# Stick-breaking scores: query parts stacked in the rows of one product, the third product side by side

## The chip, the core and the metric

The kernel runs on one core of a Trainium2 chip. What counts is its device time in microseconds (us). The time before is the median of three runs, 755.0 us (754.8 to 755.26). One further run was taken with the hardware profiler; its rows are quoted below. Engines: PE is the matrix engine (PEld is its weight loads, which overlap its products), DVE, ACT and POOL work on tiles elementwise, and SP issues most DMAs.

## The reference, cut to what matters

One decoder layer on 512 tokens and 1024 features: a norm, one wide projection, two attentions, a merge, an output projection and an FFN. The change concerns the scores of the stick-breaking attention: 8 heads of 64 features.

```python
z = jnp.einsum('bhqd,bkhd->bhqk', q_blk, k, preferred_element_type=jnp.float32) * scale
causal = kpos[None, :] < tpos[:, None]
log_keep = jnp.where(causal, jax.nn.log_sigmoid(-z), 0.0)
log_after = lax.cumsum(log_keep, axis=3, reverse=True) - log_keep
a = jnp.where(causal, jnp.exp(jax.nn.log_sigmoid(z) + log_after), 0.0)
return jnp.einsum('bhqk,bkhd->bqhd', a.astype(v.dtype), v)
```

## The kernel before

Nearly every product is made of three: a float32 operand is split into a high part in a rounded type (`float32r`) and a low part that holds the rest, and high*high, high*low and low*high are summed in PSUM (`mm3`, L161). A weight chunk of 128 x 1024 is loaded by SP, its high part is made by a copy on ACT (L147) and its low part by a subtraction on DVE (L148).

The projections come first in PE's program. `proj_feature` (L370) makes 128 features of all 512 tokens from 24 products of 512 columns, and DVE evicts them from PSUM at once (L379 and L381). `proj_token` (L384) makes values by token; for 512 columns it has four banks, two of them an "attention pair" (`take`) and two of the tag "proj". The order of the chunks is written at L644 to L659: `vs` (the values), q and k of head pair 1, of head pair 2, the six dilated chunks of the first dilated pair (`project_dil(0)`), q and k of head pair 3, then `vd0`, `vd12`, six more dilated chunks and sixteen gate chunks.

The attention runs beside this as generators that `tick` resumes after every three products. `sb_all` (L603) takes the four head pairs one after the other; each starts when its k is there and the pair ahead is through. In `sb_pair` (L436) a pair has three score groups: x (key blocks 1 and 3: 384 and 128 columns), y (key block 2: 256 columns) and z (key block 0: 512 columns). `scores` takes one of three attention pairs of PSUM banks and computes the group for both heads of the pair as plain float32 products (L441): head 0 has its 64 features in rows 0 to 63 of q and k, head 1 in rows 64 to 127, so each product uses 64 rows of the array. A mask product over all 128 rows follows (L445). `breaks` is a chain on two engines: absolute value, exponential and logarithm on ACT (L452 to L454), a sum on DVE (L455), the high part by a copy on ACT (L174) and the low part on DVE (L175). `weigh` (L469) multiplies both parts with a triangle (L472) on PE into the same banks and takes the exponential on ACT, which frees the banks; `side` (L477) multiplies with the values. POOL sums over partitions (L464) beside it. The dilated attention starts when all four pairs are done.

Each engine works through its instructions in a fixed order. Within the limits of data and buffers that order is chosen when the program is built, from priorities and an estimate of durations; q, k and the dilated chunks share 16 buffers (`NQ`).

Of the kernel before, what the change touches and what calls it, by code (L numbers as in the profile page):

```python
# [10 lines left out]
F32 = mybir.dt.float32  # L11
F32R = mybir.dt.float32r
BF16 = mybir.dt.bfloat16
AF = mybir.ActivationFunctionType
ALU = mybir.AluOpType

P = 128
S = 512
# [9 lines left out]
RAW, NQ, N4, N2, NS = 3, 16, 9, 6, 4  # L28
# [16 lines left out]
def trunk_kernel(ctx, tc, xT, gains, w_in, w_up, w_o, w_f, w_d, bias, out):  # L45
# [6 lines left out]
    V, A, G, T = nc.vector, nc.scalar, nc.gpsimd, nc.tensor  # L52
# [13 lines left out]
    def bank(tag, name):  # L66
        if tag == "proj":
            return pp.tile([P, S], F32, tag=tag, name=name, bufs=BANKS[tag])
        if ppool[1] is not None:
            return ppool[1].tile([P, S], F32, tag="att" if tag == "alpha" else "sums", name=name, bufs=BANKS["att"])  # L70
        return pair(name)[:, 0, :]
# [24 lines left out]
    for step in FFN:  # L96
        if step[0] == "in":
            i = step[1]
            chunks += [("A1", w_f[2 * i], 1024), ("S23", w_f[2 * i + 1], 1024), ("S1", None, 1024), ("S4", None, 512)]
        else:  # L100
            _, p, f = step
# [96 lines left out]
    ap_ = attp.__enter__()  # L198
# [29 lines left out]
    for k in range(KD):  # L228
# [8 lines left out]
        lo = xp.tile([P, S], F32R, tag=f"xl{k}", name=f"xl{k}")  # L237
# [5 lines left out]
    with tc.high_priority():  # L243
        weights(0)
        tc.add_manual_dep(state["last"].ins, last_split.ins.name, NOSYNC, reason="issue order")
        for x in xw:
            i = A.activation(x, x, AF.Square)
# [4 lines left out]
        V.tensor_tensor(out=xw[0], in0=xw[0], in1=xw[2], op=ALU.add)  # L252
        V.tensor_tensor(out=acc1, in0=xw[0][:, 0, :], in1=xw[0][:, 1, :], op=ALU.add)


    ident = cp.tile([P, P], F32)
    make_identity(nc, ident)
# [51 lines left out]
    def can_take():  # L309
        return min(free) <= ticks[0]  # L310
# [44 lines left out]
    def next_weights(ahead=2):  # L355
        w = weights(ci[0], ahead)
        ci[0] += 1
        return w

    def product(ps, mh_, ml_, w, nk, first=True, last=True, k0=0, between={}):  # L360
        hi, lo = w
        for k in range(nk):
            cs = slice(k * P, (k + 1) * P)
            mm3(ps, hi[:, cs], lo[:, cs], mh_[k0 + k], ml_[k0 + k], first and k == 0, last and k == nk - 1)
            tick()
            if k in between:
                with tc.high_priority():
                    between[k]()

    def proj_feature(name, scale=None, ps=None, blocks=False):  # L370
        if ps is None:
            ps = bank("proj", f"pj{name}")
            product(ps, xh, xl, next_weights(), KD)
        rb = rows["rb"]
        o = ap_.tile([P, S], F32, tag="qk", name=name, bufs=NQ)
        view = (lambda t, out=False: t.rearrange("p (c i) -> p i c" if out else "p (i c) -> p i c", c=4)) if blocks else (lambda t, out=False: t)
        with tc.high_priority():
            if scale is None:
                V.tensor_tensor(out=view(o, True), in0=view(ps), in1=view(rb), op=ALU.mult)  # L379
            else:  # L380
                V.scalar_tensor_tensor(out=view(o, True), in0=view(ps), scalar=scale, in1=view(rb), op0=ALU.mult, op1=ALU.mult)  # L381
        return o

    def proj_token(name, kind, wide_, pairs=0):  # L384

        v = ap_.tile([P, 4, wide_], F32, tag=name, name=name)
        nk = 1024 // wide_
        if wide_ == 512:
            banks = []
            for i in range(pairs):  # L390
                while not can_take():
                    tick()
                p = take(f"pv{name}{i}")
                banks += [p[:, 0, :], p[:, 1, :]]
            banks += [bank("proj", f"pv{name}{c}") for c in range(len(banks), 4)]
        else:

            b2 = [bank("proj", f"pv{name}{c}") for c in range(2)]
            banks = [b2[c // 2][:, c % 2 * wide_:(c % 2 + 1) * wide_] for c in range(4)]
        w = {}  # L400
        for j, c in [(j, c) for j in range(KD // nk) for c in range(4)]:
            if j not in w:
                w[j] = next_weights()
            ps = banks[c]
            whi, wlo = w[j]
            for i in range(nk):
                k = j * nk + i
                cs = slice(i * wide_, (i + 1) * wide_)
                mm3(ps, blk(xh[k], kind, c), blk(xl[k], kind, c), whi[:, cs], wlo[:, cs], k == 0 and (wide_ == 512 or c % 2 == 0), k == KD - 1, check=wide_ == 512)
                tick()  # L410
            if j == KD // nk - 1 and (wide_ == 512 or c % 2):
                with tc.high_priority():
                    for cc in [c] if wide_ == 512 else [c - 1, c]:
                        A.mul(v[:, cc, :], banks[cc], rows["r1"][:, 4 * kind + cc:4 * kind + cc + 1])
        for i in range(pairs if wide_ == 512 else 0):
            give(4)
        return v
# [9 lines left out]
        split_to(hi, lo, src)  # L427
        o_hi[i], o_lo[i] = hi, lo

    hs = [slice(0, 64), slice(64, 128)]  # L430

# [1 line left out]
    def sb_pair(n, q, k, v, hb, done):  # L436
        def scores(name, parts):
            ps = take(f"z{n}{name}")
            for i, (a, o) in enumerate(parts):
                for h in range(2):  # L440
                    T.matmul(ps[:, h, o:o + S - a * P], k[hs[h], a * P:(a + 1) * P], q[hs[h], a * P:], start=i == 0, stop=False, skip_group_check=True)  # L441
            for h in range(2):
                diag = ps[:, h, :].rearrange("p (a b) -> p a b", b=P)
                diag = diag[:, 0:4:3, :] if len(parts) == 2 else diag[:, 0:1, :]
                T.matmul(diag, idb, mask[:, :len(parts)], start=False, stop=False, skip_group_check=True)  # L445
            return ps
# [66 lines left out]
        f = wide(f"f{n}").rearrange("p a b -> p (a b)")[:, 256:1024]  # L513
# [3 lines left out]
        o = small(f"o{n}")  # L517
# [81 lines left out]
    vals = {}  # L599
# [18 lines left out]
            yield from dil_pair(n, [vals[f"dq{n}{g}"] for g in range(3)], [vals[f"dk{n}{g}"] for g in range(3)], lambda: vals.get("vd"))  # L618

    def project(n):  # L620
        vals[f"q{n}"] = proj_feature(f"sq{n}", 0.125)
        vals[f"k{n}"] = proj_feature(f"sk{n}")

    def project_dil(n):
        for g in range(3):
            vals[f"dq{n}{g}"] = proj_feature(f"dq{g}{n}", 0.125, blocks=g > 0)
            vals[f"dk{n}{g}"] = proj_feature(f"dk{g}{n}", blocks=g > 0)

# [2 lines left out]
    first = [pf[:, i, :] for i in range(2)]  # L631
    w = [next_weights(1 - i) for i in range(2)]
# [5 lines left out]
    def first_steps():  # L638
        yield from row_steps()
        give(3)  # L640
        vals["q0"] = proj_feature("sq0", 0.125, first[0])
        vals["k0"] = proj_feature("sk0", None, first[1])

    start(first_steps(), 14)  # L644
    start(sb_all())
    start(dil_all())
    vals["vs"] = proj_token("vs", 0, 512, 1)
    project(1)
    project(2)
    project_dil(0)  # L650
    project(3)
    vd = [proj_token("vd0", 0, 256)]
    v12 = proj_token("vd12", 1, 512, 1)
# [25 lines left out]
    for f in range(KD):  # L679
# [11 lines left out]
        lo = xp.tile([P, S], F32R, tag=f"xl{f}", name=f"ml{f}")  # L691
# [14 lines left out]
    hs = S // 2  # L706
# [35 lines left out]
    for f in HALVES:  # L742
        x = res(f)
        ps = bank("proj", f"po{f}")
# [221 lines left out]
def _layout(inputs, np):  # L966
    def feature(w, cols):
        k = w.shape[0] // P
        return w[:, cols].reshape(k, P, P).transpose(1, 0, 2).reshape(P, k * P)

    def token(w, wide):
        n = D * wide // (P * 1024)
        return list(w.reshape(n, D // (P * n), P, wide).transpose(0, 2, 1, 3).reshape(n, P, 1024))

    def fb(c0, i):
        return slice(c0 + i * P, c0 + (i + 1) * P)

    w = inputs["w_in"][0]
    ch = []
    def sb(n):  # L980
        return [feature(w, fb(0, n)), feature(w, fb(512, n))]

    def dil(n):
        return [feature(w, fb(c, 2 * g + n)) for g in range(3) for c in (1536, 2304)]

    ch += sb(0) + token(w[:, 1024:1536], 512) + sb(1) + sb(2) + dil(0) + sb(3)
    ch += token(w[:, 3072:3328], 256) + token(w[:, 3328:3840], 512) + dil(1)
    for f in range(KD):
        ch.append(feature(w, fb(3840, f)))
        ch.append(feature(w, fb(4864, f)))  # L990
    wf, wd = inputs["w_ffn_in"][0], inputs["w_ffn_out"][0]
    fch = []
    for i in range(KF):
        fch.append(feature(wf, fb(0, i)))
        fch.append(feature(wf, fb(DFF, i)))
    up = [np.concatenate([feature(inputs["w_sb_up"][0], fb(0, f)), feature(inputs["w_dil_up"][0], fb(0, f))], axis=1) for f in range(KD)]
    gains = [inputs[n].reshape(KD, P).transpose(1, 0) for n in ("norm_mix_g", "norm_ffn_g", "norm_final_g")]
    return {
        "in_xT_dram": inputs["x"][0].transpose(1, 0).reshape(KD, P, S),
        "in_gains_dram": np.concatenate(gains, axis=1),  # L1000
        "in_w_in_dram": np.stack(ch),
        "in_w_up_dram": np.stack(up),
        "in_w_out_dram": np.stack([feature(inputs["w_out"][0], fb(0, f)) for f in range(KD)]),
        "in_w_ffn_in_dram": np.stack(fch),
        "in_w_ffn_out_dram": np.stack([feature(wd, fb(0, f)) for f in range(KD)]),
    }
# [35 lines left out]
```

## Time and profile before

| | |
|---|---|
| median of three runs | 755.0 us |
| profiled execution, device time | 755.51 us |
| its span (first to last instruction) | 753.8 us |
| PE busy | 744.0 us of the span |
| DVE busy | 523.3 us |
| ACT busy | 364.9 us |
| POOL busy | 79.9 us |
| granted PE clock, mean | 0.998 of full |

The profiled execution spends 1.7 us outside its span. In a row of the timeline stand the start in us, the time from the first start to the last end in us, the engine, the line, the operation, output and inputs, the shape and the number of instructions merged. PE's products are pipelined: a row's duration holds the fill and drain, and what one costs is read from start to start.

### The profile page before, as it was taken

To read this page: it belongs to the slowest core of one execution; us is meant where nothing else is said; L and a number is where in the kernel's file an instruction comes from. 1 tells how busy PE (TensorE), PEld (TensorE's weight loads), DVE (VectorE), ACT (ScalarE), POOL (GpSimd) and SP (SyncE) were. 2 spreads that over 40 slices of the span, in tenths; PEclk is the share of its full clock that TensorE was granted. 3 is DMA by queue.
4 is the path that set the end of the run, shared out by engine and by line. 5 is a ranking of instruction groups with operands and counts; after the bars stand their busy time and mean duration, and the time that the engine had idled before them with its cause. 6 is when DMAs were issued, how large, how long until landed. Compare 5 with 4: busy or idle time off the path is not lost.

```text
span 753.8 us, 10956 instructions
## 1 busy us (share of the span) xinstructions
PE 744.0 (99%) x4447; PEld 644.2 (85%) x4447; DVE 523.3 (69%) x685; ACT 364.9 (48%) x526; POOL 79.9 (11%) x48
## 2 busy tenths in 40 slices
PE   9999999999999999999999999999999999999996
PEld 6877767788887888888888999999999999999985
DVE  6447657535887763376998989878788777776643
ACT  7255746743233533232564666545445454444453
POOL 1004043150150130000000000000000000000033
PEclk9999999999999999999999999999999999999999
DMA  8321211213232232234222233223333333332213
GB/s 266 125 83 63 79 57 57 84 56 140 85 115 110 87 110 97 70 113 159 102 75 85 92 98 105 98 84 120 99 105 98 106 99 102 106 108 70 57 57 113
DMA packets 25187, 74.13 MB, mean 98 GB/s; under 512 B 2864, under 2 KB 5936, under 8 KB 25008
## 3 DMA queue, kind: packets, MB, share of 16 engines
q1 hardware_dynamic: 23664, 69.74, 28.1%
q0 software_dynamic: 784, 3.15, 1.2%
q8 instruction: 35, 0.57, 0.3%
q10 hardware_dynamic: 688, 0.54, 0.2%
q14 instruction: 16, 0.13, 0.1%
HBM read 71.32 MB, written 2.10 MB: 97 GB/s over the span
## 4 chain that ended last, share of the span: by engine, by line
PE 93%; DVE 2%; DMA 2%; ACT 1%; issue 1%; SPq 0%; POOLq 0%; POOL 0%; DVEq 0%; ACTq 0%
PE pd L163 16%; PE pjgs L163 6%; PE pjgd L163 6%; PE pf L789 5%; PE pf L790 5%; PE pf L791 5%; PE pvvd L163 5%; PE pjdq L163 4%; PE pjdk L163 4%; PE po L163 4%; PE pg L789 4%; PE pg L790 4%; PE pg L791 4%; PE up L163 4%; PE pvvs L163 3%; PE pjsq L163 2%
## 5 line engine op out<-in xcount | busy, mean ns | idle before, releaser
L147 ACT CAST whi<-raw 128x1024 fp32r<-128x1024 f32 (+2 forms) x114 | 108.6, 954 | 160.6 <-PE pg L790 34.6
L148 DVE TENSOR_TENSOR wlo<-raw,whi 128x1024 fp32r<-128x1024 f32 (+2 forms) x114 | 138.1, 1213 | 39.9 <-ACT whi L147 39.1
L789 PE MATMUL pf<-fh,whi 128*128 128x256 f32 x348 | 98.9, 284 | 1.3 <-ACT q L796 1.3
L791 PE MATMUL pf<-fh,wlo 128*128 128x256 f32 x348 | 98.6, 283 | 0.0
L790 PE MATMUL pf<-fl,whi 128*128 128x256 f32 x348 | 98.5, 283 | 0.0
L789 PE MATMUL pg<-fh,whi 128*128 128x256 f32 x264 | 75.1, 285 | 0.6 <-ACT q L796 0.6
L790 PE MATMUL pg<-fl,whi 128*128 128x256 f32 x264 | 74.7, 283 | 0.0
L791 PE MATMUL pg<-fh,wlo 128*128 128x256 f32 x264 | 74.7, 283 | 0.0
L789 PEld LDWEIGHTS pf<-fh,whi 128*128 128x128 f32 x348 | 66.7, 192 | 2.6 <-ACT q L796 1.9
L790 PEld LDWEIGHTS pf<-fl,whi 128*128 128x128 f32 x348 | 66.7, 192 | 0.6
L791 PEld LDWEIGHTS pf<-fh,wlo 128*128 128x128 f32 x348 | 66.7, 192 | 0.3 <-DVE wlo L148 0.2
L148 DVE TENSOR_TENSOR wlo<-s,whi 128x1024 fp32r<-128x1024 f32 (+1 forms) x43 | 41.3, 960 | 15.3 <-ACT whi L147 15.2
L147 ACT CAST whi<-s 128x1024 fp32r<-128x1024 f32 (+1 forms) x43 | 36.2, 841 | 32.3 <-PE pg L790 20.5
L789 PEld LDWEIGHTS pg<-fh,whi 128*128 128x128 f32 x264 | 50.6, 192 | 1.1 <-ACT q L796 0.8
L790 PEld LDWEIGHTS pg<-fl,whi 128*128 128x128 f32 x264 | 50.7, 192 | 0.0
L791 PEld LDWEIGHTS pg<-fh,wlo 128*128 128x128 f32 x264 | 50.7, 192 | 0.0
L163 PE MATMUL pd<-hh,whi 128*128 128x512 f32 (+1 forms) x132 | 50.4, 382 | 0.0
L163 PE MATMUL pd<-hl,whi 128*128 128x512 f32 (+1 forms) x132 | 50.3, 381 | 0.0
L163 PE MATMUL pd<-hh,wlo 128*128 128x512 f32 (+1 forms) x132 | 50.1, 379 | 0.0
L892 POOL TENSOR_TENSOR inv<-inv,sq 128x256 f32<-128x256 f32 (+1 forms) x10 | 9.6, 962 | 318.1 <-ACT sq L891 315.8
L886 DVE TENSOR_TENSOR res<-pd,res 128x512 f32<-128x512 f32 (+1 forms) x36 | 22.6, 629 | 20.9 <-PE pd L163 20.8
L147 ACT CAST whi<-rawu 128x1024 fp32r<-128x1024 f32 x22 | 23.1, 1050 | 27.9 <-PE pd L163 23.7
(463 smaller groups left out, 1791.0 us busy)
## 6 DMA issues: line engine op xcount, KB each, us to landing
raw<-in_w_in_dram SPq DMA_DIRECT2D x43, 512.0 KB, 3.3
rawu<-in_w_ffn_in_dram SPq DMA_DIRECT2D x22, 512.0 KB, 3.2
raw<-in_w_ffn_in_dram SPq DMA_DIRECT2D x22, 512.0 KB, 3.3
raw<-in_w_ffn_out_dram SPq DMA_DIRECT2D x24, 384.0 KB, 3.1
raw<-in_w_out_dram SPq DMA_DIRECT2D x8, 512.0 KB, 3.3
raw<-in_w_up_dram SPq DMA_DIRECT2D x8, 384.0 KB, 2.9
x<-in_xT_dram SPq DMA_DIRECT2D x8, 256.0 KB, 4.7
res<-in_xT_dram POOLq DMA_DIRECT2D x8, 256.0 KB, 4.5
```

The source lines that it names most:

```text
L147: state["last"] = A.copy(hi[:, cs], r[:, cs])
L148: V.tensor_tensor(out=lo[:, cs], in0=r[:, cs], in1=hi[:, cs].bitcast(F32), op=ALU.subtract)
L163: return T.matmul(ps, a, b, start=start, stop=stop, skip_group_check=not check)
L789: T.matmul(ps, hi[:, cs], xhi, start=first and k == 0, stop=False, skip_group_check=True)
L790: T.matmul(ps, hi[:, cs], xlo, start=False, stop=False, skip_group_check=True)
L791: T.matmul(ps, lo[:, cs], xhi, start=False, stop=last and k == 3, skip_group_check=True)
L886: newest[1] = V.tensor_tensor(out=x, in0=ps, in1=x, op=ALU.add)
L892: G.tensor_tensor(out=rows["inv"][:, cs], in0=rows["inv"][:, cs], in1=sq[:, cs], op=ALU.add)
```

## The change

After `proj_feature` a new function `scored` makes operands of the rounded type. For q it makes two tiles, one for each head: in the head's own 64 rows the high part of q, in the other 64 rows the low part. For k it makes two tiles with the high part of the head in both halves of the rows, and one tile with the low parts of both heads. One product over 128 rows then gives k high * (q high + q low) for one head; a third product, over the 64 rows of the head, adds k low * q high. The four projections with their high and low copies add, for a head pair, four copies on ACT, two copies and four subtractions on DVE, each of 64 rows and 512 columns. Also, four of the six dilated chunks are moved ahead of q and k of pair 2, in the order of the code and in the order of the weights.

```diff
+    def scored(t, key):
+        lo = ap_.tile([P, S], F32R, tag="qk", name="klow", bufs=NQ) if key else None
+        tiles = []
+        with tc.high_priority():
+            for h in range(2):
+                own, other = hs[h], hs[1 - h]
+                y = ap_.tile([P, S], F32R, tag="qk", name=f"{'kq'[not key]}{h}", bufs=NQ)
+                A.copy(y[own], t[own])
+                if key:
+                    V.tensor_copy(y[other], y[own])
+                V.tensor_tensor(out=lo[own] if key else y[other], in0=t[own], in1=y[own].bitcast(F32), op=ALU.subtract)
+                tiles.append(y)
+        return tiles + [lo]
...
             for i, (a, o) in enumerate(parts):
                 for h in range(2):
-                    T.matmul(ps[:, h, o:o + S - a * P], k[hs[h], a * P:(a + 1) * P], q[hs[h], a * P:], start=i == 0, stop=False, skip_group_check=True)
+                    T.matmul(ps[:, h, o:o + S - a * P], k[h][:, a * P:(a + 1) * P], q[h][:, a * P:], start=i == 0, stop=False, skip_group_check=True)
+                for h in range(2):
+                    T.matmul(ps[:, h, o:o + S - a * P], k[2][hs[h], a * P:(a + 1) * P], q[h][hs[h], a * P:], start=False, stop=False, skip_group_check=True)
...
-        vals[f"q{n}"] = proj_feature(f"sq{n}", 0.125)
-        vals[f"k{n}"] = proj_feature(f"sk{n}")
-
-    def project_dil(n):
-        for g in range(3):
+        vals[f"q{n}"] = scored(proj_feature(f"sq{n}", 0.125), False)
+        vals[f"k{n}"] = scored(proj_feature(f"sk{n}"), True)
+
+    def project_dil(n, groups=range(3)):
+        for g in groups:
...
-        vals["q0"] = proj_feature("sq0", 0.125, first[0])
-        vals["k0"] = proj_feature("sk0", None, first[1])
+        vals["q0"] = scored(proj_feature("sq0", 0.125, first[0]), False)
+        vals["k0"] = scored(proj_feature("sk0", None, first[1]), True)
...
     project(1)
+    project_dil(0, [0, 1])
     project(2)
-    project_dil(0)
+    project_dil(0, [2])
     project(3)
...
-    ch += sb(0) + token(w[:, 1024:1536], 512) + sb(1) + sb(2) + dil(0) + sb(3)
+    d0 = dil(0)
+    ch += sb(0) + token(w[:, 1024:1536], 512) + sb(1) + d0[:4] + sb(2) + d0[4:] + sb(3)
```

What this does to the engines' orders is seen at three places.

**PE, scores of pair 0.** Before, they stand behind the 23rd of the 24 products that project q of pair 1 (`pjsq`); `sq` and `sk` are q and k of pair 0, and x2 is one row for the two heads.

```order
L163 MATMUL pjsq_436<-xl_172,whi_339 128x512
L441 MATMUL z0x<-sq_394,sk_396 128x384 x2
L441 MATMUL z0x<-sq_394,sk_396 128x128 x2
L445 LDWEIGHTS idb
L445 MATMUL z0x<-mask,idb 128x2x128
```

Now they begin behind the 16th product of the next chunk (`pjsk`, k of pair 1). `q_396` and `k_405` are the stacked tiles of head 0, `q_399` and `k_409` those of head 1; L458 is a product over 128 rows, L460 one over 64.

```order
L458 MATMUL z0x<-q_396,k_405 128x384
L458 MATMUL z0y<-q_396,k_405 128x256
L458 MATMUL z0z<-q_396,k_405 128x512
L163 MATMUL pjsk_530<-xl_160,whi_378 128x512
L458 MATMUL z0x<-q_399,k_409 128x384
L460 MATMUL z0x<-q_396,klow 128x384
L458 MATMUL z0y<-q_399,k_409 128x256
L460 MATMUL z0x<-q_399,klow 128x384
L458 MATMUL z0x<-q_396,k_405 128x128
L458 MATMUL z0x<-q_399,k_409 128x128
L460 MATMUL z0x<-q_396,klow 128x128
L460 MATMUL z0x<-q_399,klow 128x128
```

So the scores stand 17 products of 512 columns later, and those of pair 0 are cut apart: products over 128 and over 64 rows alternate, and those over 64 rows of x and 384 columns stand alone instead of in pairs. In pairs 1 to 3 a group stands together, as two products over 128 rows and two over 64.

**PE, the last group of pair 3.** Before, 78 rows, all products, lie between the mask of z3z and the first product that needs its high part, h3z. The piece begins with the second mask product of z3z.

```order
L445 MATMUL z3z<-mask,idb 128x128
L163 MATMUL pvvd_1069<-whi_1026,xh_159 128x256
L163 MATMUL pvvd_1069<-wlo_1027,xh_159 128x256
L163 MATMUL pvvd_1069<-whi_1026,xl_160 128x256
L163 MATMUL pvvd_1069<-whi_1026,xh_165 128x256
```

The same queue further on, around h3z and l3z (`pvvd` is the token projection, `tri` the triangle):

```order
L163 MATMUL pvvd_1272<-whi_1276,xh_159 128x512
L472 MATMUL z3z<-h3z,tri 128x512 x2
L163 MATMUL pvvd_1272<-wlo_1277,xh_159 128x512
L163 MATMUL pvvd_1272<-whi_1276,xl_160 128x512
L163 MATMUL pvvd_1273<-wlo_1277,xh_153 128x512
```

Now, from the second mask product of z3z:

```order
L464 MATMUL z3z<-mask,idb 128x128
L491 MATMUL z3x<-l3x,tri 128x512 x2
L163 MATMUL pvvd_1365<-whi_1368,xh_159 128x512
L163 MATMUL pvvd_1365<-wlo_1369,xh_159 128x512
L163 MATMUL pvvd_1365<-whi_1368,xl_160 128x512
L491 MATMUL z3y<-h3y,tri 128x256 x2
L491 MATMUL z3y<-l3y,tri 128x256 x2
L491 MATMUL z3z<-h3z,tri 128x512 x2
L491 MATMUL z3z<-l3z,tri 128x512 x2
L163 MATMUL pvvd_1363<-whi_1157,xh_129 128x512
```

Nine products are left between the mask and h3z. The rest of the token projection `vd12` that comes behind (`pvvd_1363`) goes into the attention pair of banks, of which z3x, z3y and z3z hold all three.

**DVE, the operands of pair 0.** Before, between the eviction of k of pair 0 and that of q of pair 1:

```order
L379 TENSOR_TENSOR sk_396<-first,rb_392 128x512
L148 TENSOR_TENSOR wlo_440<-raw_337,whi_439 128x1024
L381 SCALAR_TENSOR_TENSOR sq_499<-pjsq_436,rb_392 128x512
L148 TENSOR_TENSOR wlo_505<-raw_376,whi_504 128x1024
L455 SCALAR_TENSOR_TENSOR t0x<-z0x,t0x 128x1024
```

Now:

```order
L381 TENSOR_TENSOR sk_402<-first,rb_392 128x512
L148 TENSOR_TENSOR wlo_459<-raw_337,whi_458 128x1024
L399 TENSOR_TENSOR q_396<-sq_394,q_396 64x512
L399 TENSOR_TENSOR q_399<-sq_394,q_399 64x512
L398 COPY k_405<-k_405 64x512
L399 TENSOR_TENSOR klow<-sk_402,k_405 64x512
L398 COPY k_409<-k_409 64x512
L399 TENSOR_TENSOR klow<-sk_402,k_409 64x512
L383 SCALAR_TENSOR_TENSOR sq_522<-pjsq_455,rb_392 128x512
```

Six instructions of 64 rows stand between one split of weights and the next eviction; the scores of the pair wait for them. On PE everything behind the dilated chunks stands in the same order as before.

More of the change, by code (lines that the diff above doesn't have):

```diff
@@ L253, in trunk_kernel @@
         V.tensor_tensor(out=acc1, in0=xw[0][:, 0, :], in1=xw[0][:, 1, :], op=ALU.add)
+    hs = [slice(0, 64), slice(64, 128)]
     ident = cp.tile([P, P], F32)
@@ L428, in split_out @@
         o_hi[i], o_lo[i] = hi, lo
-    hs = [slice(0, 64), slice(64, 128)]
     def sb_pair(n, q, k, v, hb, done):
```

## The prediction

> **What bounds the kernel now.** I read the page first, then who waited for whom on PE, then the two stretches in which the attention runs beside the projections.
>
> ```profile
> PE 744.0 (99%) x4447; PEld 644.2 (85%) x4447; DVE 523.3 (69%) x685; ACT 364.9 (48%) x526; POOL 79.9 (11%) x48
> PE 93%; DVE 2%; DMA 2%; ACT 1%; issue 1%; SPq 0%; POOLq 0%; POOL 0%; DVEq 0%; ACTq 0%
> PE pf L789 <- ACT q L796: 1.3, 2, 0.9
> PE warm L80 <- DVE warm L77: 1.0, 1, 1.0
> PE pg L789 <- ACT q L796: 0.6, 1, 0.6
> PE first L163 <- DVE xl L187: 0.3, 1, 0.3
> 43.00:98.00 55.00, 55.00 (x263) 41.10 (x262) 35.24 (x36) 35.48 (x44) 14.49 (x3) 1.00 0.20 67
> 98.00:170.00 72.00, 72.00 (x385) 56.55 (x384) 38.70 (x42) 43.24 (x60) 23.73 (x7) 1.00 0.20 66
> ```
>
> PE is the bound: 93% of the chain that ended last is PE, and in the list of waits (us in total, times, longest) no score, triangle or value product stands. In the two stretches, which hold all of the stick-breaking attention, PE is busy throughout while DVE has 35.2 of 55 and 38.7 of 72 us, ACT 35.5 and 43.2. So every us of PE work added or saved here, and every new wait of PE, is a us of the result; copies on DVE and ACT are free as long as PE finds its operands ready.
>
> **What the scores cost.** The stretch of pair 0 with the last of the projection around it:
>
> ```profile
> 43.03 0.39 PE L163 MATMUL pjsq<-xh,whi 128*128 128x512 f32 x1
> ...
> 48.02 0.39 PE L163 MATMUL pjsq<-xl,whi 128*128 128x512 f32 x1
> 48.34 1.14 PE L441 MATMUL z0x<-sq,sk 64*128 64x384 f32 x8
> 49.41 0.39 PE L445 MATMUL z0x<-mask,idb 128*128 128x256 bf16 x2
> 49.73 0.70 PE L441 MATMUL z0y<-sq,sk 64*128 64x256 f32 x4
> 50.37 0.28 PE L445 MATMUL z0y<-mask,idb 128*128 128x128 bf16 x2
> 50.59 1.13 PE L441 MATMUL z0z<-sq,sk 64*128 64x512 f32 x4
> 51.65 0.28 PE L445 MATMUL z0z<-mask,idb 128*128 128x128 bf16 x2
> 51.74 0.48 PE L163 MATMUL pjsq<-xh,wlo 128*128 128x512 f32 x1
> 52.06 0.39 PE L163 MATMUL pjsk<-xh,whi 128*128 128x512 f32 x1
> ```
>
> A rounded product of 512 columns costs 0.227 us (22 steps in 48.02 - 43.03), 0.44 ns a column. The float32 group z0z of 512 columns takes 1.06 (50.59 to 51.65), z0y of 256 takes 0.64: 0.42 for 256 columns more, 1.64 ns a column with both heads side by side, and 0.22 fixed. Entry adds 0.09: 48.34 is 0.32 behind the product of 48.02, not 0.227. So a stretch over 64 rows costs its columns plus 0.31: weights that can't be loaded ahead (about 0.11), and a drain on each side. And a rounded product behind a mask starts its successor 0.32 later (51.74 to 52.06): 0.09 for weights not loaded ahead. Pair 0 thus cost 1.16 for x (48.25 to 49.41), 0.73 for y, 1.15 for z: 3.04 us.
>
> With the change the columns are cheap and the stretches are not. x: two products of 384 (0.34), a stretch over 64 rows (0.31 + 0.17), 0.10 for weights again, two products of 128 columns that wait for their weights (0.16), a second stretch (0.31 + 0.06): 1.45. y: 0.24 + 0.31 + 0.11 = 0.66. z: 0.45 + 0.31 + 0.22 = 0.98. Sum 3.09, against 3.04: what four passes less save goes into one more stretch over 64 rows and into products that change between 128 and 64 rows. Four pairs: +0.2. Pair 0 is cut apart besides: the two lone products of 384 columns make one stretch more (0.31), return to 128 rows once more (0.10) and don't share their columns (0.17): +0.6. Mask products ahead of stacked ones add 0.09 twice. Value products (L479) stand in seven groups instead of eight, some of them right beside scores; a group has the same 0.3 of changes, so -0.3. **PE's own work: +0.7 us.** The ends are -0.5 (all joined groups save, pair 0 costs nothing extra) and +1.5.
>
> **The operands.** 16 copies on ACT, 8 copies and 16 subtractions on DVE.
>
> ```profile
> L515 ACT ACTIVATE f<-s2x 64x512 f32<-64x512 f32 x2 | 1.3, 628 | 0.0
> L175 DVE TENSOR_TENSOR ols<-o,ohs 128x512 fp32r<-128x512 f32 x4 | 2.8, 690 | 2.4 <-ACT ohs L174 2.4
> 44.89 1.23 DVE L148 TENSOR_TENSOR wlo<-raw,whi 128x1024 fp32r<-128x1024 f32 x1 [1.04 <-ACT whi L147]
> ```
>
> At 0.63 and 0.69 that is 10.1 us of ACT and 16.6 of DVE, in stretches where ACT has 48 and DVE 53 us free. They are on PE's path only as the scores' operands. Pair 0: DVE splits weights from 44.89 for 1.23, then has six times 0.69: ready at about 50.3. PE reaches the first score 40 products behind 43.03, at 52.1: 1.8 us of cover, so they cost nothing. The DVE copy of 64 rows isn't in the trace; its bounds are 0 and the 0.69 of a subtraction, and I take 0.69. If that cover went, PE would wait for the difference.
>
> **The wait that is new.** The score groups stand later in PE's queue (pair 0 by 17 products, 3.9 us, and the pairs follow one another). In pair 3 the queue has run out of projection work that needs no attention bank. The chain that PE then waits for, z3z in the trace of before:
>
> ```profile
> 144.53 0.29 PE L445 MATMUL z3z<-mask,idb 128*128 128x128 bf16 x2
> 147.08 1.01 ACT L452 ACTIVATE t3z<-z3z 128x1024 f32<-128x1024 f32 x1
> 148.69 1.07 ACT L453 ACTIVATE t3z<-t3z 128x1024 f32<-128x1024 f32 x1
> 150.15 1.08 ACT L454 ACTIVATE t3z<-t3z 128x1024 f32<-128x1024 f32 x1
> 151.26 1.22 DVE L455 SCALAR_TENSOR_TENSOR t3z<-z3z,t3z 128x1024 f32<-128x1024 f32 x1 [0.20 <-ACT t3z L454]
> 152.88 1.05 ACT L174 CAST h3z<-t3z 128x1024 fp32r<-128x1024 f32 x1
> 154.04 1.23 DVE L175 TENSOR_TENSOR l3z<-t3z,h3z 128x1024 fp32r<-128x1024 f32 x1 [0.15 <-ACT h3z L174]
> 158.53 0.63 PE L472 MATMUL z3z<-h3z,tri 128*128 128x512 f32 x2
> ```
>
> Before, PE had 14.0 us of other work between mask (144.53) and h3z (158.53), and h3z was ready at 153.93. Now nine products stand there: two of l3x and three of the projection at 0.227, four of h3y and l3y at half of it, the mask and 0.09: about 1.75 us. The chain can't be shorter than its five links: 1.01 + 1.07 + 1.08 + 1.22 + 1.05 = 5.43, five hand-overs of 0.03 (150.15 + 1.08 to 151.26), and 0.25 from the mask's start to its result. PE stands for 5.83 - 1.75 = 4.1 us. Behind h3z comes l3z, 1.23 + 0.06 after h3z is ready, with two products (0.45) to cover: 0.8 more. Behind both, on PE, wait `pvvd_1363` and everything else; nothing is let by, so **PE loses 4.9 us**. The bounds are 4.0 (ACT or DVE somewhat quicker) and 6.5 (another copy ahead on ACT, 1.05, as before at 151.6). Freed work is not regained later: PE's order behind is the old one.
>
> **The clock.** A PE that stands long is slowed:
>
> ```profile
> L80 PE MATMUL warm<-warm 128*128 128x512 bf16 x11 | 4.9, 632 | 1.0 <-DVE warm L77 1.0
> L935 PE MATMUL warm<-warm 128*128 128x512 bf16 x8 | 2.0, 377 | 0.0
> 746.54 1.16 PE L298 MATMUL rb<-ident,r 128*128 128x128 f32 x8 [0.15 <-POOL r L909]
> 747.70:750.00 2.30, 0.00 (x1) 0.00 (x0) 1.48 (x3) 0.37 (x1) 1.28 (x1) 1.00 0.96 317
> 750.00:751.00 1.00, 0.00 (x0) 0.00 (x0) 0.00 (x0) 0.00 (x0) 0.00 (x0) 0.86 1.03 347
> 751.00:752.00 1.00, 0.00 (x0) 0.00 (x0) 0.00 (x0) 0.00 (x0) 0.00 (x0) 0.50 0.99 337
> ```
>
> PE's last product ends at 747.70; the granted clock (the third figure from the end) is 0.50 from about 750.7, 3.0 us later. At the start the eleven warm products take 0.44 each (4.9 us), the same product later 0.25 (2.0 us for eight): PE ran about 4.9 us at half clock before it was released. The wait for h3z is longer than 3.0 us, so I take it that the clock falls. Then the products behind run at half clock for some 3 to 5 us, of which part is still wait. The price lies between 0 and 2.5 (half of those 4.9 us); as 3 to 5 us at half with part of them idle I take 1.9, nearer the upper end.
>
> [...]
>
> **Sum.** Against the profiled execution: 755.5 + 0.7 + 4.9 + 1.9 = 763.0. That execution stood 0.5 above the median of the runs shown, so for the median 762.5.
>
> **Rivals.**
> - *The clock holds.* [...] 755.0 + 0.7 + 4.9 = 760.6. For it: only one fall is in the trace, at the end; against it: the wait is longer than those 3.0 us.
> - *Operands late.* While POOL sums over partitions, a DVE subtraction from SBUF stands still: the one at 65.49 takes 4.58 instead of 1.23.
>
> ```profile
> 64.46 6.13 POOL L464 PARTITION_ALL_REDUCE s0x<-t0x  x1 [27.85 <-DVE l0z L175]
> 65.49 4.58 DVE L148 TENSOR_TENSOR wlo<-raw,whi 128x1024 fp32r<-128x1024 f32 x1 [0.17 <-ACT whi L147]
> ```
>
>   The sums of a pair start when its z group is split, and now the next pair's k copies can fall into them: up to 4.4 us late (65.49 + 4.58 is 5.6 behind 64.46, less 1.2 of own work). I count some 4 us of products between, so little is lost; if 1 to 1.5 us of it were bare in pairs 1 to 3 the time would be 766.
> - *Not slower: the changes of rows are free.* Drain and bare weights belong to float32 products with their two records, and rounded ones go from 128 to 64 rows without a stop. Then a pair costs its columns: 2560 stacked and 1280 side by side at 0.44 ns, 1.7 us instead of 3.04, 5.4 us less in four pairs. With the wait of 4.9 and no fall of the clock that is 754.5. It decides if a group's saving exceeds 0.4 us on average (4.9 by 12). Against it: the entry at 48.34 costs 0.09 although the product ahead is a rounded one, and the exits to the mask cost the same. [...]
>
> **How the numbers follow.** Forecast with the fall 0.60, the clock holds 0.28, operands late 0.07, changes free 0.05. The range takes in 4.0 of wait and a low end of PE's work without a fall (759.4) and the dearest fall with the upper end of the work (764.5). Faster or slower by 0.2% (1.5 us) is about what a measurement of this kernel can tell from no change. Slower takes the first three: 0.95; the last splits into same 0.04 and faster 0.01.
>
> **What would show it.** In the profile of the changed kernel PE must wait for ACT's h3z on the triangle line, about 4 us, once, with a wait of nearly 1 for l3z behind it; the granted clock there must drop to 0.50 within 1 us of the wait's end. The scores' stretches must take near 1.4, 0.65 and 0.95 us, and no score of pair 0 may wait. The prediction is wrong if PE has work in its queue there that isn't in its order, if the stretches cost their columns only, or if waits for `klow` appear.

## The result, and the profile after

The changed kernel takes **763.24 us** (median of four runs, 762.19 to 763.65) against 755.13 for the kernel before: a ratio of 1.0104, 95% interval 1.0092 to 1.0116. It is slower by 8.1 us. The profiled execution is the lowest of the four: 762.19, with a span of 760.5 and a mean granted clock of 0.995; the other three had 0.993 or 0.994.

First the page's first part and its chain, then the list of waits of PE (us in total, times, longest), of the changed kernel:

```profile
PE 746.0 (98%) x4447; PEld 647.7 (85%) x4447; DVE 540.4 (71%) x709; ACT 375.5 (49%) x542; POOL 81.9 (11%) x48
PE 93%; DVE 3%; DMA 2%; ACT 1%; issue 1%; SPq 0%; POOLq 0%; POOL 0%; DVEq 0%; ACTq 0%
```

```profile
PE z3z L491 <- ACT h3z L174: 3.9, 1, 3.9
PE pf L809 <- ACT q L816: 1.2, 2, 0.8
...
PE z3z L491 <- DVE l3z L175: 0.6, 1, 0.6
```

PE issues as many products as before (4447) and is busy 2.0 us longer, while the span is 6.7 longer: most of the loss is PE standing. Two waits above 0.3 us are new, both on the triangle line, both in the last pair, one each. No score waits, and no wait for `klow` is there. The sum of DVE's work rose by 17.1 us and ACT's by 10.6 without showing in that list.

The timeline of PE around the wait, and that of ACT (start and length in us, engine, line, output<-input; in brackets the idle time ahead and what ended it):

```profile
158.87 0.28 PE L464 MATMUL z3z<-mask,idb 128*128 128x128 bf16 x2
...
160.45 0.40 PE L491 MATMUL z3y<-l3y,tri 128*128 128x256 f32 x2
164.79 0.73 PE L491 MATMUL z3z<-h3z,tri 128*128 128x512 f32 x2 [3.93 <-ACT h3z L174]
166.11 1.22 PE L491 MATMUL z3z<-l3z,tri 128*128 128x512 f32 x2 [0.59 <-DVE l3z L175]
167.13 0.63 PE L163 MATMUL pvvd<-whi,xh 128*128 128x512 f32 x1
...
168.84 0.48 PE L163 MATMUL pvvd<-wlo,xh 128*128 128x512 f32 x1
169.16 0.40 PE L163 MATMUL pvvd<-whi,xl 128*128 128x512 f32 x1
169.39 0.40 PE L163 MATMUL pvvd<-whi,xh 128*128 128x512 f32 x1
```

```profile
159.19 1.02 ACT L471 ACTIVATE t3z<-z3z 128x1024 f32<-128x1024 f32 x1 [3.00 <-PE z3z L464]
160.25 1.06 ACT L472 ACTIVATE t3z<-t3z 128x1024 f32<-128x1024 f32 x1
...
163.69 1.04 ACT L174 CAST h3z<-t3z 128x1024 fp32r<-128x1024 f32 x1 [1.29 <-DVE t3z L474]
```

Between the mask (158.87) and the triangle product of h3z (164.79) lie 5.92 us, nearly all of it the five links of the chain, of which the rows show the first two and the last; PE has 1.7 us of work for it (158.87 to 160.57). From 167.13 to 168.84 five projection products start 0.43 apart; from 169.16 on they start 0.23 apart again. That is the clock, in the view by stretches (from:to, length, then busy time and count of PE, PEld, DVE, ACT, POOL, the granted clock, the DMA share, GB/s):

```profile
162.17:165.59 3.42, 0.73 (x2) 0.30 (x2) 1.98 (x2) 2.13 (x4) 0.00 (x0) 1.00 0.00 0
165.50:165.70 0.20, 0.02 (x1) 0.00 (x0) 0.20 (x1) 0.20 (x2) 0.00 (x0) 0.72 0.00 0
165.59:169.00 3.41, 2.89 (x7) 2.33 (x8) 0.47 (x1) 1.57 (x3) 2.77 (x1) 0.50 0.01 2
169.00:169.20 0.20, 0.20 (x3) 0.20 (x2) 0.00 (x0) 0.00 (x0) 0.20 (x1) 1.00 0.00 0
755.90:756.30 0.40, 0.00 (x0) 0.00 (x0) 0.00 (x0) 0.00 (x0) 0.25 (x1) 0.74 1.04 335
```

A mean of 0.72 over 0.2 us is 0.09 at 1.00 and the rest at 0.50: the clock fell at 165.59, 0.8 after the wait for h3z had ended, and rose at 169.00. It was low for 3.41 us. By the last row it fell again at 756.09, at the end of the kernel, where PE has no more work.

### The profile page after: what moved, and what is told of

The parts are those of the page before. It is cut to its first block, busy times and chain, and to the rows that moved or that the text cites. A ratio compares the mean times of both kernels' runs of the same rounds, so it can differ in the third digit from the quotient of the medians.

```text
span 760.5 us, 10996 instructions
## 1 busy us (share of the span) xinstructions
PE 746.0 (98%) x4447; PEld 647.7 (85%) x4447; DVE 540.4 (71%) x709; ACT 375.5 (49%) x542; POOL 81.9 (11%) x48
## 4 chain that ended last, share of the span: by engine, by line
PE 93%; DVE 3%; DMA 2%; ACT 1%; issue 1%; SPq 0%; POOLq 0%; POOL 0%; DVEq 0%; ACTq 0%
PE pd L163 16%; PE pjgs L163 6%; PE pjgd L163 6%; PE pf L809 5%; PE pf L810 5%; PE pf L811 5%; PE pvvd L163 5%; PE pjdk L163 4%; PE pjdq L163 4%; PE po L163 4%; PE pg L809 4%; PE pg L810 4%; PE pg L811 4%; PE up L163 4%; PE pvvs L163 3%; PE pjsk L163 2%
## 5 line engine op out<-in xcount | busy, mean ns | idle before, releaser
L148 DVE TENSOR_TENSOR wlo<-raw,whi 128x1024 fp32r<-128x1024 f32 (+2 forms) x114 | 128.7, 1130 | 33.8 <-ACT whi L147 33.0
```

Of the source, the lines that this page charges most:

```text
L148: V.tensor_tensor(out=lo[:, cs], in0=r[:, cs], in1=hi[:, cs].bitcast(F32), op=ALU.subtract)
```

## The experiments

All times below are medians; "before" was run beside each group and had medians of 755.04 to 755.14.

**The parts of the change alone.** Three kernels. The first adds the operand copies to the kernel before, with nothing that reads them (`scored` ends here with `return t`, the unsplit tile):

```
-        vals[f"q{n}"] = proj_feature(f"sq{n}", 0.125)
-        vals[f"k{n}"] = proj_feature(f"sk{n}")
+        vals[f"q{n}"] = scored(proj_feature(f"sq{n}", 0.125), False)
+        vals[f"k{n}"] = scored(proj_feature(f"sk{n}"), True)
```

> The kernel before with the 16 ACT copies, 8 DVE copies and 16 DVE subtractions of the change added, whose results nothing reads; the scores are still the float32 products of before. Theory of the prediction: these operations lie beside PE and cost nothing: 755.1, within 0.2%, no new row in PE's waits. Rival 'the copies hold up the chains of the scores on ACT and DVE, and this made the wait for h3z': 757 to 760, with a wait of PE on h or l of a pair.

Measured 755.64 (11 runs; ratio 1.0005, interval 0.9996 to 1.0014). PE's waits are the old ones, but for 0.2 us in the output projection. The copies cost nothing that this can tell from zero; the interval leaves room for at most 1.1 us.

The second moves the projections in the kernel before and leaves its float32 scores:

```
+    project_dil(0, [0, 1])
     project(2)
-    project_dil(0)
+    project_dil(0, [2])
```

> The kernel before with one half of the change alone: two of the three dilated projections of pair 0 and their weights ahead of the projections of pair 2; the scores are still float32 products. Theory of the prediction: this moves products that PE issues in any case, the score groups stay where they were, and nothing waits: 755.1, within 0.2%. Rival 'the moved projections are what leaves pair 3 without cover': a wait for h3z and 759 to 763.

Measured 755.04 (11 runs; 1.0002, interval 0.9993 to 1.0011), no new wait above 0.2 us: the moved projections do nothing by themselves.

The third is the changed kernel with the two lines above in the old order:

> The other half alone: stacked query parts, the third product side by side and the operand copies, with the projections in the order of before. Theory of the prediction: the score groups of each pair come later in PE's queue because of the new operands and the cut in pair 0, so the wait for h3z and l3z (4.9) and the slow clock (about 2) are there in full: 762 to 763.5. Rival 'the wait needs the moved projections': 755 to 757.

Measured 763.07 (762.76 to 763.83; 1.0106, interval 1.009 to 1.0121). The whole loss is here. Its profiled execution (763.26) lies near the median, and so shows the clock better than the profile of the changed kernel itself. Its timeline of PE and its stretches:

```profile
165.36 1.22 PE L491 MATMUL z3z<-h3z,tri 128*128 128x512 f32 x2 [3.94 <-ACT h3z L174]
166.69 1.22 PE L491 MATMUL z3z<-l3z,tri 128*128 128x512 f32 x2
167.71 0.63 PE L163 MATMUL pvvd<-whi,xh 128*128 128x512 f32 x1
...
170.70 0.50 PE L163 MATMUL pvvd<-wlo,xh 128*128 128x512 f32 x1
171.04 0.40 PE L163 MATMUL pvvd<-whi,xl 128*128 128x512 f32 x1
```

```profile
160.68:164.09 3.41, 0.75 (x6) 0.50 (x4) 1.08 (x1) 2.23 (x3) 0.00 (x0) 1.00 0.00 0
164.09:167.50 3.41, 2.03 (x4) 1.22 (x5) 1.37 (x2) 2.46 (x3) 0.69 (x1) 0.50 0.01 2
170.80:171.00 0.20, 0.20 (x2) 0.20 (x1) 0.00 (x0) 0.00 (x0) 0.20 (x1) 0.71 0.00 0
```

Here the clock falls at 164.09, while PE still waits, and stays at 0.50 to 170.92 (0.71 over the last row): 6.83 us, twice 3.41. From 167.71 to 170.70 lie seven steps from product to product, 0.43 each.

**Cover for the chain.** The changed kernel, with the last dilated pair's projections put where PE runs out of work:

```
+    project_dil(1)
     v12 = proj_token("vd12", 1, 512, 1)
     vals["vd"] = vd + [v12[:, :, 0:256], v12[:, :, 256:512]]
-    project_dil(1)
...
-    ch += token(w[:, 3072:3328], 256) + token(w[:, 3328:3840], 512) + dil(1)
+    ch += token(w[:, 3072:3328], 256) + dil(1) + token(w[:, 3328:3840], 512)
```

> The changed kernel with the projections of the last dilated pair (and their weights) placed ahead of the value projection of the dilated branch, so that PE has more products between z3z's mask and z3z's triangle product. Theory of the prediction: the wait of 4.9 and the fall of the clock go, PE's own work (+0.7) stays: 755.1 + 0.7 = 755.8, no wait of PE for h3z or l3z, clock 1.00 to the end. Rival 'PE's own work in the stacked and 64-row products is dearer than counted and carries the loss': 760 or more. Rival 'the wait moves elsewhere' (to another pair's h, to the softmax of the dilated pairs): 760 to 763, with a new row in PE's waits.

Measured 754.75 (11 runs; 0.9994, interval 0.9985 to 1.0003). The waits for h3z and l3z are gone and none above 0.2 us took their place; the stretch that held them is full. The row of this kernel:

```profile
158.00:164.70 6.70, 6.70 (x33) 5.55 (x32) 3.60 (x4) 5.72 (x7) 0.00 (x0) 1.00 0.16 64
```

It is 1 us below what the theory expected, so the same order was given to the kernel before:

> The kernel before, with only the projections of the last dilated pair and their weights placed ahead of the value projection, as in the kernel of the cover. It tells what this order is worth by itself, so that the cover's 754.75 can be read. Theory of the prediction (PE's own work of the change is +0.7): the order itself saves about 1 us, since groups of 64-row products stand elsewhere, and this gives 754.0. Rival 'the change costs PE nothing': the order is worth nothing, 755.0, and the cover's 754.75 is the whole own work, -0.3.

Measured 754.66 (11 runs; 0.9992, interval 0.9984 to 1.0001): 0.5 below before, which its interval doesn't quite tell from no change, and between the two expectations. In this order the change costs PE 754.75 - 754.66 = 0.1 us, which the intervals don't tell from zero.

**The clock alone.** Products of zeros keep PE busy through the wait, without moving its end:

```
-        def weigh(ps, hi, lo, new):
+        def weigh(ps, hi, lo, new, zeros=0):
...
+            for i in range(zeros):
+                T.matmul(ps[:, i % 2, :], warm, warm.unsqueeze(1).to_broadcast([P, 2, P]), start=False, stop=i >= zeros - 2, skip_group_check=True)
...
-        ey = weigh(*by)
+        ey = weigh(*by, zeros=30 if n == 3 else 0)
```

> The changed kernel, with 30 bf16 products of zeros with 256 columns (0.11 us each, 3.3 us) added to the bank of z3y after the triangle products of y of pair 3, where PE otherwise stands for h3z; they add nothing to the scores. Theory of the prediction: the chain Abs, Exp, Ln, score, cast still ends when it did, so the wait for h3z shrinks from 4 us to below 1 us and the products after it come no earlier, but the granted clock stays at 1.00: only the price of the slow clock goes, 1.9 by the prediction's term, so about 761.3 against the 763.2 of the changed kernel. Rival 'the clock costs nothing here' (its slow stretch lies within the waits): 763.2. Rival 'the wait isn't set by that chain but by what PE issues ahead': the zero products push it, 766.

Measured 760.22 (760.16 to 760.57; 1.0068, interval 1.0055 to 1.0081). Its timeline of PE:

```profile
160.75 3.45 PE L493 MATMUL z3y<-warm 128*128 128x256 bf16 x30
164.85 0.73 PE L491 MATMUL z3z<-h3z,tri 128*128 128x512 f32 x2 [0.65 <-ACT h3z L174]
166.18 0.73 PE L491 MATMUL z3z<-l3z,tri 128*128 128x512 f32 x2 [0.60 <-DVE l3z L175]
166.75 0.40 PE L163 MATMUL pvvd<-whi,xh 128*128 128x512 f32 x1
166.99 0.39 PE L163 MATMUL pvvd<-wlo,xh 128*128 128x512 f32 x1
```

The triangle product comes when it came before (164.85 against 164.79), the products behind it start 0.24 apart, and the kernel is 3.0 us faster for 30 useless products. That is 1.1 more than expected, and not all of it is the clock: in this profile PE waits 0.3 for `pf` in the feed-forward part, where the changed kernel waits 1.2. So up to 0.9 came there. Nor is the order of PE's products the old one behind the wait: one projection product now stands between the value products of pair 3, at 172.13, and the stretch of projections takes 0.5 more than in the next kernel, which keeps the changed kernel's order on every engine. That one has half as many zeros (`zeros=15`):

> The changed kernel with 15 instead of 30 products of zeros behind z3y's triangle products of pair 3: the wait for h3z is about 2.3 us long instead of 3.9 (changed kernel) or 0.6 (30 products), and ends at the same time. Theory of the prediction (the clock falls where PE stands longer than the 3.0 us seen at the kernel's end): the clock holds, 760.2 as with 30. [...]

Measured 760.31 (759.8 to 761.81; 1.007, interval 1.0057 to 1.0083). Of five executions four had 759.8 to 760.4 and a mean clock of 0.997 or 0.998, one 761.81 and 0.995. The median is the expected 760.2; the outlier is 1.5 above it, and since it has no trace, what lowered its mean clock isn't shown. The profile (760.06) is one with the clock kept, at 1.00 through the wait of 2.3 us and behind it, and these are rows of its timeline of PE and its stretches:

```profile
160.73 1.81 PE L493 MATMUL z3y<-warm 128*128 128x256 bf16 x15
164.82 0.72 PE L491 MATMUL z3z<-h3z,tri 128*128 128x512 f32 x2 [2.28 <-ACT h3z L174]
...
167.90 0.39 PE L163 MATMUL pvvd<-whi,xl 128*128 128x512 f32 x1
```

```profile
160.73:164.15 3.42, 1.81 (x17) 1.38 (x15) 1.23 (x1) 2.10 (x3) 0.00 (x0) 1.00 0.00 0
164.15:167.56 3.41, 2.13 (x8) 1.67 (x9) 1.23 (x1) 2.67 (x4) 1.29 (x1) 1.00 0.01 2
```

The product of 167.90 is the one that the changed kernel started at 169.16, in the same place of the same order: 1.26 us is what the slow clock cost in that profile. The 0.3 at `pf` is in this profile too; why is open, and wasn't tried further.

The changed kernel once more:

> The changed kernel once more, unaltered, for a second look at the slow clock. In its first profile (762.2, the lowest of four times) the granted clock was 0.50 from about 165.6 to 169.0 and cost 1.2 us; the other three times were 0.9 to 1.5 higher at the same program. Theory: where the fall begins changes from execution to execution, so that more of the slow stretch lies on products; the median stays near 763.2, and a profile near the median shows a slow stretch that costs about 2 us. Rival: the difference between the times comes from another place (a wait in the feed-forward part); then the slow stretch costs 1.2 again and another wait is longer.

Measured 762.94 (762.12 to 763.49, four runs). The profile was again of the lowest (762.12) and shows what the first showed: a wait of 3.9, and a clock at 0.50 from 164.84 to 168.26, again 3.4 us. So it doesn't show directly what the dearer executions do; their mean clock of 0.993 is that of the profile with 6.8 us above.

**Shorter waits.** The changed kernel, with the two 64-row parts of x behind its two stacked parts:

```
                     T.matmul(ps[:, h, o:o + S - a * P], k[h][:, a * P:(a + 1) * P], q[h][:, a * P:], start=i == 0, stop=False, skip_group_check=True)
+            for a, o in parts:
                 for h in range(2):
                     T.matmul(ps[:, h, o:o + S - a * P], k[2][hs[h], a * P:(a + 1) * P], q[h][hs[h], a * P:], start=False, stop=False, skip_group_check=True)
```

> The changed kernel with the two 64-row parts of the score group x behind its two stacked parts, in the changed kernel's own order of projections. PE's order around pair 3 comes out so that the wait is cut in two: about 2.3 + 0.4 for h and l of z3y and 2.2 + 0.7 for those of z3z, none of them as long as the 3.0 us after which the clock fell at the end of the kernel. Theory: the waits still cost their 5.6 us, the clock holds: 752.5 (cover and grouping together) + 5.6 = 758.1, and no clock below 1.00 in the stretch. Rival 'the clock falls after shorter waits too': 2 to 3 more, 760 to 761.

Measured 762.07 (761.38 to 762.41; 1.009, interval 1.0076 to 1.0104). This expectation failed, and the time is above the rival's range too. The waits came out nearly as foreseen (2.1 and 0.3 for z3y, 2.0 for h3z), but the clock fell, for 6.8 us. Stretches of this kernel:

```profile
158.28:161.69 3.41, 1.01 (x4) 0.59 (x4) 1.85 (x3) 2.91 (x4) 0.00 (x0) 1.00 0.00 0
161.40:162.00 0.60, 0.18 (x2) 0.00 (x0) 0.60 (x1) 0.00 (x0) 0.00 (x0) 0.74 0.00 0
162.00:163.40 1.40, 0.00 (x0) 0.00 (x0) 0.45 (x1) 0.92 (x1) 0.00 (x0) 0.50 0.00 0
168.50:169.00 0.50, 0.50 (x4) 0.50 (x3) 0.00 (x0) 0.00 (x0) 0.50 (x1) 0.98 0.00 0
```

The clock fell at 161.69 (0.74 over 0.6 us), though PE had never stood for more than 2.1 at a time. In the 3.41 us ahead of that, PE was idle for 3.41 - 1.01 = 2.4.

**Two versions that beat both kernels.** Cover and grouping together:

> The kernel of the cover, and in the score group x the two 64-row parts behind the two stacked parts, so that x has one 64-row stretch instead of two. Theory of the prediction: a stretch costs 0.31 beside its columns; four pairs save one each, pair 0 somewhat more: 1.2 to 2 us less than the cover alone, so 753.8 to 754.6, within 0.2% of before or just under it. Rival 'changes of rows cost nothing for rounded products': the same as the cover alone, 755.8. Rival 'the grouping delays x's result and opens a wait for h3x or h3y': over 757.

Measured 752.51 (0.9966, interval 0.9954 to 0.9978), 2.2 below the cover alone; the theory had said 1.2 to 2. The group x of pair 1 in the changed kernel, and then in this one:

```profile
83.08 0.62 PE L458 MATMUL z1x<-q,k 128*128 128x384 f32 x2
83.64 0.45 PE L460 MATMUL z1x<-q,klow 64*128 64x384 f32 x2
84.01 0.44 PE L458 MATMUL z1x<-q,k 128*128 128x128 f32 x2
84.38 0.33 PE L460 MATMUL z1x<-q,klow 64*128 64x128 f32 x2
84.64 0.39 PE L464 MATMUL z1x<-mask,idb 128*128 128x256 bf16 x2
```

```profile
82.12 0.79 PE L458 MATMUL z1x<-q,k 128*128 128x384 f32 x4
82.84 0.50 PE L461 MATMUL z1x<-q,klow 64*128 64x384 f32 x4
83.28 0.39 PE L465 MATMUL z1x<-mask,idb 128*128 128x256 bf16 x2
```

From the first stacked product to the mask 1.56 became 1.16: one more stretch over 64 rows and the return from it cost 0.40, for the same columns.

And the cover with the lower key part stacked in both halves of the rows too, so that no score runs over 64 rows:

```
+                lo = ap_.tile([P, S], F32R, tag="qk", name=f"klow{h}", bufs=NQ) if key else None
                 V.tensor_tensor(out=lo[own] if key else y[other], in0=t[own], in1=y[own].bitcast(F32), op=ALU.subtract)
+                if key:
+                    V.tensor_copy(lo[other], lo[own])
+                    los.append(lo)
...
-        return tiles + [lo]
+        return tiles + [los]
...
-                    T.matmul(ps[:, h, o:o + S - a * P], k[2][hs[h], a * P:(a + 1) * P], q[h][hs[h], a * P:], start=False, stop=False, skip_group_check=True)
+                    T.matmul(ps[:, h, o:o + S - a * P], k[2][h][:, a * P:(a + 1) * P], q[h][:, a * P:], start=False, stop=False, skip_group_check=True)
```

> The kernel of the cover, with the lower part of the keys also stacked in both halves of the rows (8 more DVE copies of 64 rows), so that the third product runs over 128 rows against both query parts and no score is a 64-row product; the result gains the product of the two lower parts. Theory of the prediction: a 64-row stretch costs 0.31 beside its columns, 17 of them in four pairs (5.3 us); against that the columns of the two heads no longer run side by side, 1280 more in a pair at 0.44 ns (2.3 us in four pairs, and some for products of 128 columns): 2 to 3.5 us less than the cover, 751.3 to 752.8. Rival 'changes of rows cost rounded products nothing': 2.3 us more than the cover, 757. Rival 'the further copies come too late': a wait of PE on klow, over 755.

Measured 751.57 (0.9952, interval 0.9938 to 0.9965), 3.2 below the cover, in the expected range. It streams some 4700 columns more than the cover (1280 in a pair, less the 384 that pair 0 streamed apart in any case) and is faster: here side by side in 64 rows saves less in columns (2.1 us at 0.44 ns) than the changes of rows take.

## Why the prediction came out right

**The sum.** From the first product that projects q of pair 1 (`pjsq`) to the last product of the projections (`pjgd`) PE took 273.6 us before and 280.4 after. The last product of before, in its view by tile (least, median and longest duration in ns, then first and last start in us), and then the first and the last one in the timeline of the changed kernel:

```profile
L163 PE MATMUL pjgd<-xh,wlo x64: 388/389/398, 227.7 to 316.6; 128*128 128x512 f32 x64
```

```profile
42.47 0.39 PE L163 MATMUL pjsq<-xh,whi 128*128 128x512 f32 x1
...
322.91 0.39 PE L163 MATMUL pjgd<-xh,wlo 128*128 128x512 f32 x1
```

316.6 - 43.03 = 273.6 and 322.91 - 42.47 = 280.4: the loss of 6.8 of this execution lies wholly in there. The terms follow.

**The wait, 4.9: right.** The h3z product comes 164.79 - 160.57 = 4.2 behind the product ahead of it (the second of the two at 160.45), 0.12 of which is that product's own: 4.1, as predicted. For l3z PE stood 0.6 by the list and lost 0.8 to 0.9 between the starts (1.32 from 164.79 to 166.11, less two products). The chain has the five links and the length that the trace of before gave. That it is the queue's position that lost the cover, and not a slower chain, is shown by the cover: the same stacked products with other work in that place wait for nothing. Why the mask of z3z comes so late is less clear than the prediction has it. The prediction explains it by the 17 products of pair 0, 3.9 us, handed on from pair to pair. But in the traces the mask of z3x is 5.5 later (140.11, now 145.64), that of z3y 9.8 (142.38, now 152.19) and that of z3z 14.3 (144.53, now 158.87), while the place of h3z moved only from 158.53 to 160.57. So most of the lost cover was lost inside pair 3. What pushes the groups back there, the operands or the cut through pair 0, wasn't separated.

**The clock, 1.9: right in size, its reason wrong.** In the profile with 6.8 us of low clock the products of l3z start 1.02 ahead of the next product, against 0.57 with the clock kept; seven steps of 0.43 stand in place of 0.235; one more lost 0.1: 0.45 + 1.35 + 0.1 = 1.9. In the first profile of the changed kernel, with 3.4 us of low clock, it is 1.3 by the same count, in the second 0.9, and these were the cheapest executions of their groups. So the size varies from execution to execution, and that 1.9, chosen between 0 and 2.5, meets the one profile near a median is in part luck. The 3 to 5 us at half clock behind it were the author's estimate, and so was the half clock of the first 4.9 us, read from 0.44 us a product against 0.25 (the clock in the view of before is 1.00 there); the traces show 3.41 us in the changed kernel, 3.4 when it ran once more, 6.83 in the third kernel and 6.8 with the shorter waits. What failed is the reason given: that PE must stand longer than 3.0 us at a stretch. With waits of 2.1 and 2.0 the clock came down too.

In the three profiles with one long wait and a slow stretch, all with a wait of 3.9, the clock fell 1.3 us before the wait's end (164.09, third kernel), at its end (164.84, the changed kernel once more) or 0.8 after it (165.59). In the 3.41 us ahead of the fall PE was idle for 2.7 in the changed kernel (162.17 to 165.59, 0.73 busy) and 3.4 when it ran once more, 2.7 in the third kernel (160.68 to 164.09) and 2.4 with the shorter waits. With 15 zeros PE stood 2.3 and then 0.6, and the clock stayed at 1.00. What sets the moment of the fall, and whether it lasts 3.4 us or 6.8, these runs don't show. The clock fell in both executions of the changed kernel that were profiled, and the six others have a mean clock of 0.993 or 0.994, lower than either (0.995 and 0.997).

**PE's own work, +0.7: right in this order, by errors that are small.** 6.8 less 4.9 and 1.3 leaves 0.6. The stretch of x in pair 1 came out at 1.56 (predicted 1.45). The rest stands at its beginning: from 83.08 to 83.64 the two products of 384 columns take 0.56, where 0.34 for columns and 0.09 for the entry make 0.43. In the rows of z1x of the changed kernel each product behind a change of rows starts 0.06 to 0.08 before the modelled end of the row ahead (83.64 against 83.08 + 0.62), a projection product behind another 0.17 (169.39 against 169.16 + 0.40): that much less overlap is what the traces show of the drain in the prediction. Its weights not loaded ahead stand in the trace of before, where the load for z0x starts at 48.34 together with the product and that of the projection product of 48.02 at 47.80, 0.22 ahead. The groups y and z of pair 3 took 0.64 (151.55 to 152.19) and 0.99 (157.88 to 158.87), predicted 0.66 and 0.98. In the order of the cover the own work is 0.1, not 0.7, by runs whose intervals are wider than that: so this term may belong to an order of the queue and not to the change alone, and that its total came out is not proof of each of its parts.

**The operands, nothing: right.** Added without their readers they are not to be told from zero, and in the changed kernel pair 0's last lower key part is ready 2.2 us ahead of the first score (1.8 predicted). A timeline of DVE and one of PE, changed kernel:

```profile
48.19 0.42 DVE L398 CAST k<-k 64x512 fp32r<-64x512 f32 x1
48.64 0.69 DVE L399 TENSOR_TENSOR klow<-sk,k 64x512 fp32r<-64x512 f32 x1
```

```profile
51.55 0.33 PE L458 MATMUL z0x<-q,k 128*128 128x384 f32 x1
```

The copy of 64 rows, which no row of before showed, takes 0.42 and not the 0.69 that was taken for it.

**What is left.** At the median 755.1 + 0.6 + 4.9 + 1.9 make 762.5. The 0.7 up to 763.2 are not placed; they lie outside the projections, if the profile of the third kernel (763.26) stands for the median: its stretch from `pjsq` to `pjgd` is 281.0, and 7.4 more than before is the sum of the terms. The ends of the range don't follow from those of the terms: 755.0 + 4.0 - 0.5 is 758.5 and not 759.4, and 755.0 + 4.9 + 2.5 + 1.5 is 763.9 and not 764.5. Both ranges hold what was measured.

**The rivals.** "The clock holds" named 760.6; with the clock kept by zeros the kernel takes 760.2, so its price came close, helped by up to 0.9 at `pf` that no term foresaw, but the clock of the changed kernel fell to 0.50. "Operands late" fell: the longest subtraction for `klow` took 4.9 us, and no product waited for one.

```profile
L399 DVE TENSOR_TENSOR klow<-sk,k x8: 683/1652/4908, 47.5 to 141.8; 64x512 fp32r<-64x512 f32 x8
```

"Changes of rows are free" fell twice: x came out at 1.56, and taking changes away, by grouping or by full rows, saved 2.2 and 3.2 us. The 0.09 that the prediction held against this rival couldn't decide it, for the same 0.09 stands behind a mask (51.74 to 52.06), where the rows don't change.

## What to carry to other kernels

Where PE is the bound, look at the chain of the other engines behind each product and count the work that stands in PE's queue up to its answer: here an edit that left PE's own work nearly alone took away the cover of one chain, in one of four pairs, and lost 5 us there. A wait can cost more than its length: around the end of the one of 3.9 us here the clock was at 0.50 for 3.41 us, which cost 1.3, and 1.9 in the profile where it was low for 6.83. Useless products in the wait took 3.0 us off the kernel, and work that is needed anyway 8.5. Weigh fewer columns against changes between 128 and 64 rows: here 0.40 us for one more change paid for some 900 columns.

## What was not expected of the hardware

- Breaking the wait up did not keep the clock here. With waits of 2.1, 0.3 and 2.0 in place of the one of 3.9 it fell to 0.50 for 6.8 us, and one wait of 2.3 us, in the kernel with 15 zeros, left it at 1.00 in the execution that was profiled.
- The same program had its clock at 0.50 for 3.4 us in the two executions that were profiled, and in the six others a mean clock of 0.993 or 0.994, where the profile with 6.83 us of it has 0.993: one profile can show 0.9 or 1.3 of a price that is nearer 1.9 at the median.
- In the two kernels with products of zeros at 160 us, the profile shows a wait of 0.3 instead of 1.0 to 1.5 at `pf`, 250 us later. Its cause stays open.
